# Branch C's output gate and a 512-column block of the output projection, each as seven quarter products with the tokens stationary

## The chip, the core and the metric

The kernel runs on one core of one Trainium2 chip. A core has five engines that run their own queues side by side: TensorE (PE, matrix products into the PSUM banks), VectorE (DVE), ScalarE (ACT), GpSimd (POOL) and SyncE (SP, which here issues the loads). Each engine takes its instructions strictly in the order in which the scheduler left them, and semaphores make one wait for another. The metric is the device time of the whole program in microseconds (us), the median of several executions.

## What is computed

Two layers, each a residual mixer over 512 tokens of width 1024. One input projection feeds four token mixers (branches A to D); each branch is multiplied by its own gate, projected up and merged by sigmoid gates; an output projection and a residual add follow. Cut to what matters here:

```
for l in range(2):
    h = rmsnorm(x, norm_g[l])                    # 512 x 1024
    proj = h @ w_in[l]                           # all branch inputs and gates
    c = sigmoid(o_raw) * mlstm(q, k, v, i, f)    # o_raw: 512 columns of proj, branch C's output gate
    c = headwise_rmsnorm(c) * silu(z_c)
    m = sum_n sigmoid(gate_n) * (y_n @ w_branch[l, n])
    x = x + m @ w_out[l]                         # 1024 x 1024
out = rmsnorm(x, final_g)
```

## The kernel before

Every product is done in float32r with both operands split in a high part (a rounding copy, on ScalarE) and a low part (the rest, a subtraction on VectorE). `mm3` issues three matmuls for it: high by high, high by low, low by high. Weights come in units of 128x1024 (512 KB) through `Stream`: a raw buffer `wr` (three of them), then the high part `wh` (line 283 or 257) and the low part `wl` (line 293 or 260), four buffers each. `Stream.get` keeps the loads five units ahead.

Three forms of product occur. `proj_W` (line 376) takes four units of 256 rows by 512 columns and accumulates four PSUM banks of 128 tokens by 512 columns: 4 units x 4 token tiles x 2 row tiles x 3 = 96 matmuls of 128x512. `proj_N` (line 359) does 256 columns with two units, 4 x 8 x 3 = 96 matmuls of 128x256. The merge gates already use seven quarter products (Strassen-Winograd): for these `split7` (line 249) makes the sums of the weight quarters on VectorE (lines 266 to 269), and `combine` (line 923) makes sums of the quarters of the normalised tokens, `bq`: T1, T2, T4 (split at lines 943 and 944) and T3 (written over a quarter of the tokens themselves by `in_place`, lines 955 and 956). Branch C's output gate runs as a `proj_W` on the four units of `co`, and `use_o` takes each of its banks in with one tanh on ScalarE (line 1001) and one update of `hC` on VectorE (line 1002). It comes behind branch D's q/k block and its v block (copied out at line 980), and `combine` runs beside it. The lines 1377 to 1422 are branch D: transposes, scores, products with the values.

The output projection takes the merged `mp` (split at lines 1058 and 1059) with a `proj_W` for columns 0 to 511 (taken in at line 1456) and two `proj_N` for the rest.

The order on each engine comes from the scheduler: program order, with the work under `high_priority` (weight casts, the taking in of results) put first, and side jobs released by `pump` as TensorE work is issued. Tiles come from pools (PSUM: four banks `pm`, four `px`), so a product also waits until the bank it takes has been read.

## Time and profile before

| | us |
|---|---|
| median of 3 runs (lowest to highest) | 1304.38 (1304.19 to 1304.83) |
| the profiled execution | 1304.66 |
| its span, first to last instruction | 1302.5 |
| TensorE busy in the span | 1294.3 (99%) |
| VectorE busy | 979.0 (75%) |
| ScalarE busy | 655.1 (50%) |
| granted TensorE clock, mean share of full | 0.999 |

In the timelines a row is: start in us from the start of the span, duration, engine, line of the kernel, operation, output and inputs by the program's names, shapes, count, and in brackets how long the engine had been idle and what released it. Instructions of one engine overlap a little, so the time that one takes in a full queue is the distance from start to start, not the duration. In the windows each engine has its busy time within the stretch, then the granted clock and what the transfers did.

### The profile page before, as it was taken

The page shows a single profiled execution, that of the slowest core. Times are in us where ns is not written, and L with a number is a line of the kernel's source. Part 1 is how long each engine was busy: PE and PEld are TensorE (multiplying, and loading weights), DVE is VectorE, ACT ScalarE, POOL GpSimd, SP SyncE. Part 2 cuts the span into 40 slices and gives each one's busy share as a digit, 9 for nine tenths or more (in the row PEclk, how much of TensorE's full clock was granted, in tenths as well). Part 3 has the DMA queues.
Part 4 walks back from the last instruction along what each step waited for, and adds up shares of the span by engine and source line. Part 5 has one row for each costly group of instructions (what it writes and reads, how often), then busy time and mean ns, then how long its engine had stood idle before and what let it go on. Part 6 is the DMA issues. An engine that isn't in the chain of part 4 may idle for free.

```text
span 1302.5 us, 20320 instructions
## 1 busy us (share of the span) xinstructions
PE 1294.3 (99%) x8044; PEld 1147.6 (88%) x8044; DVE 979.0 (75%) x1670; ACT 655.1 (50%) x1204; POOL 22.6 (2%) x35
## 2 busy tenths in 40 slices
PE   9999999999999999999999999999999999999998
PEld 9878888888999999998997788888889999999987
DVE  6676968876778797886476778798857787878855
ACT  6479323235457566454443973231454565764433
POOL 1000000000000001000000000000000000100000
PEclk9999999999999999999999999999999999999999
DMA  6222242211233233325432323332203233233341
GB/s 241 89 86 97 85 142 91 88 49 50 97 104 107 98 113 100 97 98 192 133 106 83 110 84 104 124 97 78 69 17 130 82 118 108 84 98 102 111 177 66
DMA packets 42191, 133.62 MB, mean 103 GB/s; under 512 B 5336, under 2 KB 5592, under 8 KB 42096
## 3 DMA queue, kind: packets, MB, share of 16 engines
q1 hardware_dynamic: 39504, 128.06, 29.3%
q10 hardware_dynamic: 2592, 4.27, 0.9%
q8 instruction: 63, 1.03, 0.3%
q14 instruction: 32, 0.26, 0.1%
HBM read 128.06 MB, written 4.24 MB: 102 GB/s over the span
## 4 chain that ended last, share of the span: by engine, by line
PE 95%; ACT 1%; DVE 1%; DMA 1%; issue 0%; POOL 0%; POOLq 0%; ACTq 0%
PE pm L337 23%; PE pm L338 23%; PE pm L339 23%; PE px L337 5%; PE px L339 5%; PE px L338 5%; PE px L1254 1%; DMA wr<-in_wu_dram 1%; PE px L1013 1%; PE px L1412 1%; ACT wh L257 1%; PE pm L543 1%; DVE wl L260 1%; PE px L1332 1%; PE px L1307 1%; PE px L1348 0%
## 5 line engine op out<-in xcount | busy, mean ns | idle before, releaser
L337 PE MATMUL pm<-hn,wh 128*128 128x512 f32 (+1 forms) x704 | 243.1, 345 | 0.0
L338 PE MATMUL pm<-hn,wh 128*128 128x512 f32 (+1 forms) x704 | 241.8, 344 | 0.0
L339 PE MATMUL pm<-hn,wl 128*128 128x512 f32 (+1 forms) x704 | 241.8, 343 | 0.0
L283 ACT CAST wh<-wr 128x1024 fp32r<-128x1024 f32 (+1 forms) x136 | 142.3, 1048 | 179.7 <-PE pm L339 75.1
L293 DVE TENSOR_TENSOR wl<-wr,wh 128x1024 fp32r<-128x1024 f32 (+1 forms) x136 | 166.1, 1223 | 79.8 <-ACT wh L283 79.7
L257 ACT CAST wh<-wr 128x1024 fp32r<-128x1024 f32 x120 | 125.3, 1047 | 110.5 <-DVE wr L268 72.1
L260 DVE TENSOR_TENSOR wl<-wr,wh 128x1024 fp32r<-128x1024 f32 x120 | 146.6, 1223 | 29.2 <-ACT wh L257 29.0
L337 PEld LDWEIGHTS pm<-hn,wh 128*128 128x128 f32 x704 | 132.5, 188 | 19.6 <-ACT cv L639 0.7
L338 PEld LDWEIGHTS pm<-hn,wh 128*128 128x128 f32 x704 | 132.6, 188 | 18.0 <-issue 0.4
L339 PEld LDWEIGHTS pm<-hn,wl 128*128 128x128 f32 x704 | 132.5, 188 | 16.8
L337 PE MATMUL pm<-wh,hn 128*128 128x512 f32 (+2 forms) x352 | 130.7, 372 | 0.0
L338 PE MATMUL pm<-wl,hn 128*128 128x512 f32 (+2 forms) x352 | 128.4, 365 | 0.0
L339 PE MATMUL pm<-wh,hn 128*128 128x512 f32 (+2 forms) x352 | 128.3, 365 | 0.0
L339 PE MATMUL pm<-yh,wl 128*128 128x512 f32 x256 | 101.1, 395 | 0.0
L337 PE MATMUL pm<-yh,wh 128*128 128x512 f32 x256 | 101.0, 394 | 0.0
L338 PE MATMUL pm<-yl,wh 128*128 128x512 f32 x256 | 100.9, 394 | 0.0
L337 PE MATMUL px<-T,wh 128*128 128x256 f32 x320 | 90.8, 284 | 0.9 <-ACT tg L1116 0.6
L339 PE MATMUL px<-T,wl 128*128 128x256 f32 x320 | 90.1, 281 | 0.0
L338 PE MATMUL px<-T,wh 128*128 128x256 f32 x320 | 89.8, 281 | 0.0
L339 PEld LDWEIGHTS pm<-wh,hn 128*128 128x128 f32 x352 | 66.2, 188 | 11.3
L338 PEld LDWEIGHTS pm<-wl,hn 128*128 128x128 f32 x352 | 66.3, 188 | 10.6 <-DVE wl L293 0.2
L337 PEld LDWEIGHTS pm<-wh,hn 128*128 128x128 f32 x352 | 66.2, 188 | 10.2
(352 smaller groups left out, 2834.2 us busy)
## 6 DMA issues: line engine op xcount, KB each, us to landing
wr<-in_wu_dram SPq DMA_DIRECT2D x212, 512.0 KB, 3.5
row<-rows SPq DMA_DIRECT2D x24, 256.0 KB, 4.1
x<-in_x_dram SPq DMA_DIRECT2D x15, 256.0 KB, 5.5
wr<-in_wz_dram SPq DMA_DIRECT2D x4, 544.0 KB, 4.6
xs<-x ACTq DMA_DIRECT2D x8, 256.0 KB, 2.6
x<-xs SPq DMA_DIRECT2D x8, 256.0 KB, 5.4
out_dram<-xo SPq DMA_DIRECT2D x4, 256.0 KB, 2.1
out_dram<-xo ACTq DMA_DIRECT2D x4, 256.0 KB, 2.5
```

What stands on the lines that cost most here:

```text
L257: A.copy(w[0], s)
L260: V.tensor_tensor(w[1], s, w[0].bitcast(F32), ALU.subtract)
L283: h = A.copy(hi, raw)
L293: d = V.tensor_tensor(lo, raw, hi.bitcast(F32), ALU.subtract)
L337: mm(ps, lh, rh, start=first, stop=False, **kw)
L338: mm(ps, lh, rl, start=False, stop=False, **kw)
L339: lastpm[0] = mm(ps, ll, rh, start=False, stop=last, **kw)
L543: pin(mm(bank[t][:, :272], xn[t, h][:, j * P:(j + 1) * P], ws.raw[h][:, 272 * j:272 * j + 272], start=h == 0 and j == 0, stop=h == 1 and j ...
L1013: nc.tensor.transpose(ps[:, t * P:(t + 1) * P], y[t][:, j * P:(j + 1) * P], ident)
L1254: mm(two(py, t)[:, 64 * e:64 * e + 64], M[e][:, t, :], xdt[t][:, o:o + 64], start=True, stop=True)
L1307: mm(ps[:, t], kT[h][:, s], qT[h][:, s], start=True, stop=True)
L1332: mm(pi[:, i], Ps[h][:, t], v1[t][:, h], start=True, stop=True)
```

## The change

The output gate of branch C and columns 256 to 767 of the output projection go through a new helper, `seven_w`. It views a 1024x512 block of weights as four quarters of 512x256 (one unit each, new unit kinds `in7w` and `out7w`) and the tokens as four quarters of 256 tokens by 512 rows, and computes seven products of 2 x 4 x 3 = 24 matmuls of 128x256, with the token quarters stationary. The four weight sums (S1 to S4) and all seven splits of weights are made inside it, from the raw units; before, four units were split as they came. X is one `px` bank used five times; three products add into what a bank holds already, and each partial result is taken in under high priority: a copy, then additions.

For the gate, the token sums are those of `combine`. For the projection, new sums of `md` (four subtractions of 128x256 for each of four row tiles) and their splits are made ahead of it. The projection's first 256 columns now come first as a `proj_N`, the middle 512 in seven products, the last 256 as a `proj_N` as before. There are four raw buffers `wr` in place of three, and four tiles `tm` in place of five. `in_place` comes right after `combine`, ahead of the gate.

The diff, cut to its core:

```
-    wide("dq", "dv", "co")
+    wide("dq", "dv")
+    wide7("in7w", OFF["co"])
...
-    for q in range(4):
-        u.append(("out4", 0, q))
-    for b in range(2, 4):
-        for h in range(2):
-            u.append(("out", 256 * b, h))
+    for h in range(2):
+        u.append(("out", 0, h))
+    wide7("out7w", 256)
+    for h in range(2):
+        u.append(("out", 768, h))
...
-    NTM = 5
+    NTM = 4
...
-                    raw = wp.tile([P, n], F32, name=nm("wr"), tag="wr", bufs=3)
+                    raw = wp.tile([P, n], F32, name=nm("wr"), tag="wr", bufs=4)
...
+    def seven_w(bq, acc):
+        a, b_, c_, d = ws.raw[-4:]
...
+        def part(n_, raw):
+            with tc.high_priority():
+                hi = wp.tile([P, 1024], F32R, name=nm("wh"), tag="wh", bufs=4)
+                lo = wp.tile([P, 1024], F32R, name=nm("wl"), tag="wl", bufs=4)
+                A.copy(hi, raw)
+                V.tensor_tensor(lo, raw, hi.bitcast(F32), ALU.subtract)
+            w[n_] = (hi, lo)
...
+        def product(ps, n_, t_, first):
+            for t in range(2):
+                for k in range(4):
+                    s, o = slice(t * P, (t + 1) * P), slice(k * 256, (k + 1) * 256)
+                    mm3(ps[:, t], bq[t_][0][k][:, s], bq[t_][1][k][:, s], w[n_][0][:, o], w[n_][1][:, o],
+                        first and t == 0 and k == 0, k == 3, skip_group_check=True)
...
+        part("A11", a)
+        sums(c_, c_, d, ALU.add)
+        sums(a, c_, a, ALU.subtract)
+        part("A12", b_)
+        sums(b_, b_, a, ALU.subtract)
+        part("S2", a)
+        part("S1", c_)
+        X = psx([P, 2, 256])
+        Y = [psm([P, 2, 256]) for _ in range(2)]
+        product(X, "A11", "B11", True)
+        take_in(0, 0, X, False)
+        sums(c_, d, a, ALU.subtract)
+        part("S3", c_)
+        product(Y[0], "A12", "B21", True)
+        take_in(0, 0, Y[0], True)
+        part("S4", b_)
+        product(X, "S2", "T2", False)
+        take_in(0, 1, X, False)
+        part("A22", d)
+        product(Y[1], "S1", "T1", True)
+        take_in(1, 1, Y[1], False)
+        product(X, "S3", "T3", False)
+        take_in(1, 1, X, True)
+        product(Y[1], "S4", "B22", False)
+        take_in(0, 1, Y[1], True)
+        product(X, "A22", "T4", False)
+        take_in(1, 0, X, True)
...
         for _ in steps:
             pass
+        in_place()
         yTA = halves(yA)
-        proj_W(hn, use_o)
+        seven_w(bq, use_o)
...
-        proj_W(mp, use_out0)
...
+        for k in range(4):
+            x, y = md[k], md[4 + k]
+            V.tensor_tensor(x[:, u0], x[:, u1], x[:, u0], ALU.subtract)
+            V.tensor_tensor(x[:, u1], y[:, u1], x[:, u1], ALU.subtract)
+            V.tensor_tensor(y[:, u1], y[:, u1], x[:, u0], ALU.subtract)
+            V.tensor_tensor(y[:, u0], y[:, u0], y[:, u1], ALU.subtract)
...
+        proj_N(mp, use_out0)
+        seven_w(bo, use_out7)
```

Where the instructions now stand, at three places of the first layer. First VectorE beside branch C's output gate, from the weight split that the anchor of the prediction is to the first T1. `bq` are the token sums, the T rows their low parts, `wl` low parts of weights, `qk` branch D's rotation, `to` and `hC` the gate's taking in. Before:

```order
408 L293 TENSOR_TENSOR wl_2504<-wr_2501,wh_2503 128x1024 [waits DMAHW2_49,PE_49,Activation_49]
409 L934 TENSOR_TENSOR bq_2541<-hn_120,hn_121 128x512
410 L938 TENSOR_TENSOR bq_2535<-bq_2537,bq_2535 128x512 [waits DVE_49]
411 L1383 TENSOR_TENSOR qk_2260<-qk_2260,cst_sb 128x256 [waits PE_49]
412 L938 TENSOR_TENSOR bq_2537<-bq_2541,bq_2537 128x512 [waits DVE_49]
413 L944 TENSOR_TENSOR T_491_2548<-bq_2535,T_490_2547 128x512 [waits Activation_49]
414 L938 TENSOR_TENSOR bq_2541<-bq_2541,bq_2535 128x512 [waits DVE_49]
415 L1383 TENSOR_TENSOR qk_2273<-qk_2273,cst_sb 128x256 [waits PE_49]
416 L938 TENSOR_TENSOR bq_2539<-bq_2539,bq_2541 128x512 [waits DVE_49]
417 L944 TENSOR_TENSOR T_493_2552<-bq_2541,T_492_2551 128x512 [waits Activation_49]
```
After (S3's weight sum stands one row ahead of this piece):

```order
413 L1005 TENSOR_TENSOR bq_2519<-bq_2521,bq_2519 128x512
414 L1464 TENSOR_TENSOR qk_2260<-qk_2260,cst_sb 128x256 [waits PE_49]
415 L1005 TENSOR_TENSOR bq_2521<-bq_2525,bq_2521 128x512 [waits DVE_49]
416 L329 TENSOR_TENSOR wl_2671<-wr_2457,wh_2670 128x1024 [waits Activation_49]
417 L1076 TENSOR_TENSOR to_2633<-to_2633,pm_2607 128x512 [waits PE_49]
418 L1023 TENSOR_TENSOR hn_121<-bq_2521,hn_120 128x2x256 [waits Activation_49]
419 L329 TENSOR_TENSOR wl_2712<-wr_2408,wh_2711 128x1024 [waits Activation_49]
420 L1083 SCALAR_TENSOR_TENSOR hC_2310<-to_2633,hC_2310 128x256 [waits Activation_49]
421 L269 TENSOR_TENSOR wal_2912<-wr_2901,wah_2911 128x512 [waits DMAHW3_49]
422 L1083 SCALAR_TENSOR_TENSOR hC_2378<-to_2633,hC_2378 128x256
423 L1005 TENSOR_TENSOR bq_2525<-bq_2525,bq_2519 128x512
424 L1011 TENSOR_TENSOR T_483_2532<-bq_2519,T_482_2531 128x512
```
T_491 before and T_483 after are the low part of T1's first half. Before, three rows of 512 and one of 256 stand between the weight split and it; after, S3's and S4's low parts, an accumulation `to`, two updates of `hC`, `in_place`'s row and the next merge gate's split stand there as well.

Second, TensorE where it first takes a token sum. Before, in the first merge gate:

```order
1314 L338 MATMUL pm_2940<-hn_121,wh_2674 128x256
1315 L339 MATMUL pm_2940<-hn_120,wl_2675 128x256
1316 L337 MATMUL pm_2941<-T_490_2547,wh_2678 128x256 [waits Activation_49]
1317 L338 MATMUL pm_2941<-T_491_2548,wh_2678 128x256
1318 L339 MATMUL pm_2941<-T_490_2547,wl_2679 128x256 [waits DVE_49]
```
After, in the middle of branch C's output gate:

```order
1257 L404 MATMUL px_2606<-wh_2598,T_484_2535 128x256 [waits Activation_49]
1258 L405 MATMUL px_2606<-wl_2599,T_484_2535 128x256
1259 L404 MATMUL pm_2608<-wh_2602,T_482_2531 128x256
1260 L405 MATMUL pm_2608<-wl_2603,T_482_2531 128x256
1261 L406 MATMUL px_2606<-wh_2598,T_485_2536 128x256 [waits DVE_49]
1262 L404 MATMUL px_2606<-wh_2598,T_484_2535 128x256
1263 L405 MATMUL px_2606<-wl_2599,T_484_2535 128x256
1264 L406 MATMUL px_2606<-wh_2598,T_485_2536 128x256
1265 L406 MATMUL pm_2608<-wh_2602,T_483_2532 128x256
1266 L404 MATMUL pm_2608<-wh_2602,T_492_2555 128x256 [waits Activation_49]
1267 L405 MATMUL pm_2608<-wl_2603,T_492_2555 128x256
1268 L406 MATMUL pm_2608<-wh_2602,T_493_2556 128x256 [waits DVE_49]
```
T_482 and T_483 are T1's first half, T_484 and T_485 T2's, T_492 and T_493 T1's second half. What stood behind the gate now stands inside it, with nothing else of TensorE's between.

Third, VectorE in the output projection, around the first taking in of results. Before:

```order
788 L293 TENSOR_TENSOR wl_6167<-wr_6164,wh_6166 128x1024 [waits DMAHW7_49,Activation_49]
789 L293 TENSOR_TENSOR wl_6197<-wr_6194,wh_6196 128x1024 [waits DMAHW0_49,Activation_49]
790 L293 TENSOR_TENSOR wl_6227<-wr_6224,wh_6226 128x1024 [waits DMAHW1_49,Activation_49]
791 L1456 TENSOR_TENSOR x_6141<-x_6141,pm_6160 128x512 [waits PE_49]
792 L1456 TENSOR_TENSOR x_6145<-x_6145,pm_6161 128x512 [waits PE_49]
793 L1456 TENSOR_TENSOR x_6149<-x_6149,pm_6162 128x512 [waits DMAHW3_49,PE_49]
```
After (px_6422 is the product A11, pm_6423 the product A12, wl_6415 the low part of S2, the wr rows the weight sums):

```order
830 L1544 TENSOR_TENSOR x_6228<-x_6228,px_6422 128x256 [waits PE_49]
831 L1544 TENSOR_TENSOR x_6232<-x_6232,px_6422 128x256
832 L334 TENSOR_TENSOR wr_6295<-wr_6295,wr_6297 128x1024 [waits DMAHW7_49,DMAHW0_49]
833 L334 TENSOR_TENSOR wr_6071<-wr_6295,wr_6071 128x1024 [waits DVE_49]
834 L1544 TENSOR_TENSOR x_6228<-x_6228,pm_6423 128x256 [waits PE_49]
835 L334 TENSOR_TENSOR wr_6160<-wr_6160,wr_6071 128x1024 [waits DVE_49]
836 L329 TENSOR_TENSOR wl_6415<-wr_6071,wh_6414 128x1024 [waits Activation_49]
837 L329 TENSOR_TENSOR wl_6419<-wr_6295,wh_6418 128x1024 [waits Activation_49]
```
Before, the weight splits stand ahead of all additions; after, the sums that S1 and S2 are made of stand behind additions that wait for TensorE.

## Rows read from the trace of the kernel before

**Rows 1.** Page: busy time, share of span, instructions; then the chain's shares by engine
```profile
PE 1294.3 (99%) x8044; PEld 1147.6 (88%) x8044; DVE 979.0 (75%) x1670; ACT 655.1 (50%) x1204; POOL 22.6 (2%) x35
...
PE 95%; ACT 1%; DVE 1%; DMA 1%; issue 0%; POOL 0%; POOLq 0%; ACTq 0%
```

**Rows 2.** Timeline of TensorE, output projection and ahead: start us, duration, line, shapes
```profile
603.80 0.28 PE L337 MATMUL px<-T,wh 128*128 128x256 f32 x1
...
605.22 0.40 PE L337 MATMUL pm<-yh,wh 128*128 128x512 f32 x1
...
608.01 0.39 PE L337 MATMUL pm<-wh,mph 128*128 128x512 f32 x1
...
630.21 0.28 PE L337 MATMUL pm<-wh,mph 128*128 128x256 f32 x1
```

**Rows 3.** Windows, first layer: length; PE, PEld, DVE, ACT, POOL busy; clock; transfers' share, GB/s
```profile
275.00:280.00 5.00, 5.00 (x27) 4.12 (x26) 1.94 (x4) 2.12 (x3) 0.00 (x0) 1.00 0.14 55
280.00:285.00 5.00, 5.00 (x28) 4.21 (x27) 5.00 (x10) 2.89 (x5) 0.00 (x0) 1.00 0.30 108
...
295.00:300.00 5.00, 5.00 (x23) 4.03 (x22) 4.90 (x8) 3.96 (x7) 0.00 (x0) 1.00 0.31 102
300.00:305.00 5.00, 5.00 (x35) 4.54 (x34) 5.00 (x8) 4.71 (x15) 0.00 (x0) 1.00 0.09 20
```

**Rows 4.** Timeline of VectorE, gate stage; last bracket: idle before, released by
```profile
278.13 1.23 DVE L293 TENSOR_TENSOR wl<-wr,wh 128x1024 fp32r<-128x1024 f32 x1 [3.06 <-ACT wh L283]
279.27 0.68 DVE L934 TENSOR_TENSOR bq<-hn,hn 128x512 f32<-128x512 f32 x1
...
280.48 0.42 DVE L1383 TENSOR_TENSOR qk<-qk,cst_sb 128x256 f32<-128x256 f32 x1
280.81 0.68 DVE L938 TENSOR_TENSOR bq<-bq,bq 128x512 f32<-128x512 f32 x1
281.42 0.68 DVE L944 TENSOR_TENSOR T<-bq,T 128x512 fp32r<-128x512 f32 x1
...
294.24 0.69 DVE L944 TENSOR_TENSOR T<-bq,T 128x512 fp32r<-128x512 f32 x1
...
299.19 1.29 DVE L944 TENSOR_TENSOR T<-bq,T 128x512 fp32r<-128x512 f32 x2
...
306.00 1.29 DVE L1389 TENSOR_TENSOR dqs<-dqT,cstd_sb 128x512 f32<-128x512 f32 x2 [0.70 <-ACT dqT L1379]
...
921.38 1.23 DVE L293 TENSOR_TENSOR wl<-wr,wh 128x1024 fp32r<-128x1024 f32 x1 [3.03 <-ACT wh L283]
```

**Rows 5.** Timeline of TensorE, gate stage, the same columns
```profile
276.36 0.40 PE L337 MATMUL pm<-wh,hn 128*128 128x512 f32 x1
...
279.17 1.47 PE L1377 MATMUL px<-cst_sb,qk 128*128 128x128 f32 x12
...
300.50 0.28 PE L337 MATMUL pm<-hn,wh 128*128 128x256 f32 x1
...
301.94 0.29 PE L337 MATMUL pm<-T,wh 128*128 128x256 f32 x1
...
307.95 0.49 PE L1412 MATMUL px<-vD,In 128*128 128x128 f32 x2
```

**Rows 6.** Timeline of ScalarE, gate stage, the same columns
```profile
276.56 0.59 ACT L980 COPY vD<-pm 128x512 f32<-128x512 f32 x1 [0.81 <-PE pm L339]
```

**Rows 7.** Windows, first layer, output projection, the same columns
```profile
615.00:620.00 5.00, 5.00 (x23) 4.05 (x22) 1.13 (x1) 0.65 (x1) 0.00 (x0) 1.00 0.35 111
620.00:625.00 5.00, 5.00 (x23) 4.03 (x22) 1.23 (x1) 0.48 (x2) 0.00 (x0) 1.00 0.33 111
```

**Rows 8.** End of the run: TensorE's last matmul, then two windows behind it
```profile
1296.25 0.28 PE L339 MATMUL pm<-wh,mpl 128*128 128x256 f32 x1
...
1297.00:1299.00 2.00, 0.00 (x0) 0.00 (x0) 1.12 (x3) 1.07 (x3) 0.55 (x1) 1.00 0.67 254
1299.00:1300.00 1.00, 0.00 (x0) 0.00 (x0) 0.00 (x0) 0.16 (x1) 0.00 (x0) 0.55 0.21 76
```

## What the change does to the time

> **What bounds the kernel now.** I read the page's busy shares and chain first [rows 1]. TensorE is busy for 99% of the span and 95% of the chain of work that ended last is its own, so one microsecond less of TensorE work is one microsecond less of time, as long as nothing else becomes late. Then I read the two stages that the change touches, in order of time, because VectorE's 75% is an average. From 280 to 305 us, which is the whole of branch C's output gate, VectorE is full: five windows of 5 us each hold 4.90 to 5.00 us of work [rows 3], while the window ahead has 1.94. In the output projection it has room: 1.13 and 1.23 of 5 us [rows 7]. The second layer runs the same code 643 us later (921.38 for 278.13 in [rows 4]), so each term is worked out for the first layer and taken twice.
>
> **TensorE's own work falls.** 96 matmuls of 128x512 run from 608.01 to 630.21, which is 0.2313 us each; 12 of 128x256 run from 603.80 to 605.22, 0.1183 each [rows 2]. Either stage goes from 96 x 0.2313 = 22.2 us to 7 x 24 = 168 matmuls x 0.1183 = 19.9 us. That is -2.3 us per stage, four times, -9.3 us in all if nothing waits. The other two column blocks of the projection keep their form and only change places.
>
> **Output gate: what moves.** The seven products need the token sums T1 to T4, which `combine` makes. Before, the first matmul with a T starts at 301.94 [rows 5], after the gate. Now it is the 49th of the gate's matmuls. In the trace of before, T1's low part is ready in two halves, at 281.42 and 294.24 (plus 0.68), and the second half of T2 only in the pair from 299.19 [rows 4]. So even the unchanged queue would hand T2 over as the gate ends. The new queue of VectorE is longer still, and in the first pair of order rows above, the low parts of the weight sums S3 and S4, an accumulation and two gate updates stand ahead of the first T1.
>
> I walk that queue with start-to-start times of back-to-back instructions: 1.14 us for 1024 elements (278.13 to 279.27), 0.61 for 512 (280.81 to 281.42), 0.33 for 256 (280.48 to 280.81) [rows 4]. The anchor is the low part at 278.13, which waits 3.06 us for ScalarE's cast; that cast stands behind the copy of branch D's last values at 276.56, which waits for TensorE [rows 6]. Its counterpart in the new queue stands behind the same copies, so I leave the anchor there. From it to T1's first half there are four instructions of 1024 elements, seven of 512 and three of 256: 4.6 + 4.3 + 1.0 = 9.9 us. T1's first half then starts at 288.0 and is done at 288.7, where before it started at 281.42. Ten more of 512 and two of 256, and one short wait of about 0.6 for ScalarE's cast between, lead to T1's second half, done near 295.9; T2's second half follows near 298.1.
>
> TensorE starts the gate at 276.36 and has the transposes of branch D (1.47 us) among its first products [rows 5]: A11 and A12 are 48 x 0.1183 = 5.7, so it is through at 276.36 + 5.7 + 1.5 = 283.5. Then it is in order: S1·T1 and S2·T2 (the second pair of order rows). It waits from 283.5 to about 289 for the first halves, works 12 matmuls (1.4 us), waits again until about 295 for the second half of T1, works 20 more, waits shortly for T2, and does the last 15. It is through at 298.1 + 15 x 0.1183 = 299.9. Of the 16.4 us, 48 matmuls are 5.7, so **about 10.7 us are waits**. S3·T3 adds into the bank that S2·T2 left, and has to wait for ScalarE's copy of it: by a copy's 0.59 [rows 6] and the end of the matmul, 1.0. Then 72 matmuls are 8.5. The stage ends at 309.4, where before the next one started at 300.50 [rows 5]: **+8.9**, the saving of 2.3 included.
>
> Behind it a smaller loss follows. The tanh of the last quarter, the casts of the next weights and the copies of branch D's transposes all stand behind the last product on ScalarE. Before, TensorE had 24 matmuls of 256 and 10 of 512 columns to do between 300.50 and branch D's scores; now 11 of them are free to run there. Walked the same way, branch D's next product, at 307.95 before [rows 5], starts 8.4 us later with 3.0 us less done ahead of it. So this costs 2.5 us more (bounds 0, and 5.2, all the work that stood there), and **the gate loses 11.4 us per layer**. The bounds are +7.2, the added length of VectorE's queue from the anchor to 306.00 (nine of 1024, 33 of 512, eleven of 256, 33.9 us by the rates above, against five, 33 and three, 26.7), and +14, with every wait at its end. The remaining weight sums stand earlier, where VectorE works 1.94 of 5 us just ahead of the gate [rows 3]; I cost them at nothing, and at 1 us where the load of the fourth unit would come late.
>
> **Clock.** The trace of before has one row on it: the last matmul starts at 1296.25, the granted clock is 1.00 in the window from 1297 to 1299 and 0.55 in the next [rows 8], so with TensorE idle it has gone from 2.4 towards 1.2 GHz. The first wait here is about 5.3 us and the second about 4, and either could end at the lower level. No matmul of before runs at the lower level, so I bound the price: 0 if the level is back before the last T arrives, since the slow matmuls ahead of that only fill a wait; 87 matmuls x 0.1183 = 10.3 us if it stays for the rest of the stage. I take the 15 matmuls after T2 at double time, **+1.8 per layer**, near the low end, since the slowed matmuls between the waits come for free. The Trainium skill's page "TensorE: Matmul & The Clock Gate", section "HAM oscillation — how this bites in real kernels", speaks against this change: groups of matmuls with waits between them each start at half rate. By it the full second and third group are slow, and the price nears the upper half of my bounds; no row of before shows it.
>
> **Output projection.** The 256-column block now comes first (96 x 0.1183 = 11.4 us from 608.01), then A11 and A12, to 625.1. VectorE has room, but its order counts (third pair of order rows): the sum of units c and d, two more sums and the splits of S2 and S1 stand behind additions that wait for A11 (622.2) and A12. From A11's end: two additions of 256, two sums of 1024 to about 625.6, ScalarE's cast of S2 to 627.0, that of S1 to 628.1, the low part of S2 to 628.4. TensorE, through with A12 at 625.4 after 0.35 for the last merged columns, starts S2·T2 in full at 628.4, some 2.9 us late with a few tenths more after it: +3.4 - 2.3 = **+1.1 per layer** (bounds -2.3, everything hidden, and +3). The splits of the token sums there lie beside the first block, in VectorE's free time.
>
> **The sum.** 11.4 + 1.8 + 1.1 = 14.3 per layer, 28.6 for two. The profiled execution took 1304.66 us, 0.3 over the median of the runs, so the forecast is 1304.7 + 28.6 = **1333 us**.
>
> **Rivals.** (a) *Only VectorE's added length counts*: if the waits for the T overlap with what came behind, the clock holds and the projection breaks even, the loss is 7.2 per layer: 1319. For it: TensorE has work of the next stage that needs no T. Against it: that work stands behind the products in TensorE's order. (b) *The clock stays low* after T2 in each gate stage, at 6.8 to 10.3 us per layer in place of 1.8: 1343 to 1350. For it speaks the row of the end [rows 8]; against it that after 298 matmuls run without long waits. By the rule of the Trainium skill's page named above, this is the case to expect. (c) *All of it is hidden*, and the time falls to 1304.7 - 9.3 = 1295. Place: the wait ahead of S1·T1. Its point is T1 and T2 complete by about 286 us, when TensorE gets to their second halves. The 281.42 of T1's first half in before speaks for it, the 294.24 and 299.19 of the second halves [rows 4] and the full windows [rows 3] against it. (d) *Gate and projection cancel out*: the projection gains its 4.6 and the gate loses about as much, near 1304. It needs a gate that loses 2 us per layer, below its lower bound.
>
> **How the numbers follow.** My forecast 0.55, (a) 0.20, (b) 0.13, (c) 0.08, (d) 0.04. The range reaches down to 1315, a little under (a), and up to 1349, most of (b). About 0.2% (2.6 us) is what a measurement can tell from no change. Faster by more: 0.08, within: 0.04, slower: 0.88.
>
> **What would show it.** TensorE's waits in the gate stage: two long ones on VectorE's T1 low part, of about 5 and 4 us, at 283 and 290 us and again 650 us later; first matmul of branch D's second product near 316; a granted clock below 1 just behind them; in the projection a wait of near 3 us ahead of S2·T2, released by ScalarE's cast. VectorE's windows from 280 to 310 full. If the waits for T1 are under 2 us, the walk of the queue is wrong, and with it the sign.

## The result, and the profile of the changed kernel

The changed kernel takes **1332.79 us** (median of 4 runs, 1332.28 to 1333.27) against 1304.29 for the kernel before in the same comparison (4 runs, 1303.89 to 1304.83). The ratio is 1.0218, with a 95% interval of 1.0202 to 1.0233. It is slower by 28.5 us; the forecast was 28.6. The profiled execution took 1332.83 us, with a span of 1330.9 and a mean granted clock of 0.987.

The page answers [rows 1] with busy time, share and count of each engine, and the chain's shares by engine:

```profile
PE 1299.1 (98%) x8332; PEld 1166.3 (88%) x8332; DVE 1037.9 (78%) x1780; ACT 676.7 (51%) x1238; POOL 22.5 (2%) x35
...
PE 93%; DVE 6%; ACT 1%; DMA 0%; issue 0%; POOLq 0%; POOL 0%
```

VectorE has gone from 1% to 6% of the chain that sets the end. TensorE's busy time is 4.8 us up, although its matmuls were to take 9.3 us less: part of them ran at the lower clock. And its idle time has gone up by 23.6 (28.4 of span less 4.8). The view of TensorE's waits says for whom (waiting operation and line, releaser and line: us in total, times, longest); the largest in the kernel before was 1.1:

```profile
PE pm L406 <- DVE T L1011: 9.7, 2, 4.9
PE pm L404 <- ACT T L1010: 6.3, 2, 3.2
PE px L404 <- ACT wh L328: 3.1, 2, 1.5
...
PE px L404 <- ACT to L1072: 1.4, 2, 0.7
PE pm L404 <- ACT wh L328: 1.1, 2, 0.6
PE px L1493 <- DVE In L1485: 0.9, 2, 0.5
```

The T are the token sums of the output gate; each wait occurs twice, once per layer. L328 is the cast of a weight sum; 2 x (1.5 + 0.6) us of waits on it belong to the output projection. Now TensorE's timeline in the gate of the first layer, which answers [rows 5] (start, duration, line, operands; in brackets the idle time before and its releaser):

```profile
283.84 0.28 PE L404 MATMUL pm<-wh,T 128*128 128x256 f32 x1
...
289.10 0.58 PE L406 MATMUL pm<-wh,T 128*128 128x256 f32 x1 [4.86 <-DVE T L1011]
...
294.90 0.58 PE L404 MATMUL pm<-wh,T 128*128 128x256 f32 x1 [3.16 <-ACT T L1010]
...
296.17 0.42 PE L404 MATMUL pm<-wh,T 128*128 128x256 f32 x1
296.39 0.41 PE L405 MATMUL pm<-wl,T 128*128 128x256 f32 x1
...
300.65 0.37 PE L404 MATMUL px<-wh,T 128*128 128x256 f32 x1
300.86 0.28 PE L405 MATMUL px<-wl,T 128*128 128x256 f32 x1
300.98 0.28 PE L406 MATMUL px<-wh,T 128*128 128x256 f32 x1
...
303.00 0.39 PE L404 MATMUL px<-wh,hn 128*128 128x256 f32 x1 [0.68 <-ACT to L1072]
...
311.64 0.28 PE L404 MATMUL pm<-hn,wh 128*128 128x256 f32 x1
...
318.33 0.49 PE L1493 MATMUL px<-vD,In 128*128 128x128 f32 x2 [0.45 <-DVE In L1485]
```

Two long waits at the T's, a short one for ScalarE's copy of S2·T2, and the gate ends at 311.64 where it ended at 300.50 before. Between 296.17 and 300.65 matmuls start 0.21 us apart, from 300.86 on 0.12: the first stretch ran at the lower clock. VectorE over the same time, which answers [rows 4]:

```profile
278.60 1.23 DVE L329 TENSOR_TENSOR wl<-wr,wh 128x1024 fp32r<-128x1024 f32 x1 [3.01 <-ACT wh L328]
...
288.37 0.68 DVE L1011 TENSOR_TENSOR T<-bq,T 128x512 fp32r<-128x512 f32 x1
...
295.06 0.68 DVE L1011 TENSOR_TENSOR T<-bq,T 128x512 fp32r<-128x512 f32 x1
...
297.47 0.68 DVE L1011 TENSOR_TENSOR T<-bq,T 128x512 fp32r<-128x512 f32 x1
```

After the anchor there is no bracket in these rows, so VectorE worked without a pause; T1's first half came at 288.37 because that is where it stood in the queue. The windows, which answer [rows 3] (length; busy time of PE, PEld, DVE, ACT, POOL; granted clock; transfers):

```profile
285.00:290.00 5.00, 0.90 (x4) 0.90 (x5) 5.00 (x9) 2.13 (x5) 0.00 (x0) 0.72 0.62 210
290.00:295.00 5.00, 1.84 (x9) 1.48 (x8) 5.00 (x10) 0.92 (x2) 0.00 (x0) 0.50 0.00 0
295.00:300.00 5.00, 4.90 (x21) 4.61 (x22) 3.84 (x7) 1.85 (x3) 0.00 (x0) 0.50 0.00 0
300.00:305.00 5.00, 4.32 (x33) 4.12 (x32) 2.41 (x3) 4.20 (x7) 0.00 (x0) 0.92 0.30 100
```

From 285 to 295 TensorE works 2.7 of 10 us while VectorE works all ten. Before, TensorE was full on both sides of this stretch [rows 3]. From 290 to 300 the granted clock is 0.50, the 1.2 GHz level.

To cut the 28.4 us into stages, the starts of the first and the last matmul with `mph` in the output projection, in both layers, are compared between profiles. Rows of after:

```profile
620.46 0.28 PE L404 MATMUL pm<-wh,mph 128*128 128x256 f32 x1
...
669.32 0.28 PE L405 MATMUL pm<-wl,mph 128*128 128x256 f32 x1
...
1277.28 0.28 PE L404 MATMUL pm<-wh,mph 128*128 128x256 f32 x1
...
1324.51 0.28 PE L405 MATMUL pm<-wl,mph 128*128 128x256 f32 x1
```

And of the kernel before, whose first one, 608.01, stands in [rows 2]:

```profile
654.32 0.28 PE L338 MATMUL pm<-wl,mph 128*128 128x256 f32 x1
...
1251.40 0.39 PE L337 MATMUL pm<-wh,mph 128*128 128x512 f32 x1
...
1296.13 0.28 PE L338 MATMUL pm<-wl,mph 128*128 128x256 f32 x1
```

The lag is 620.46 - 608.01 = 12.45 us when the first projection begins and 15.00 when it ends, so the first layer's gate with all behind it costs 12.45 and the projection 2.55. In the second layer it is 10.88 and 2.50. The same four rows, read in every run's profile, give this table (us; the experiments are told below):

| kernel | median, us | over before | to projection 1 | projection 1 | to projection 2 | projection 2 |
|---|---|---|---|---|---|---|
| the change | 1332.79 | 28.5 | +12.45 | +2.55 | +10.88 | +2.50 |
| e1 gate alone | 1328.81 | 24.3 | +12.17 | +0.12 | +11.75 | -0.14 |
| e2 projection alone | 1307.52 | 3.0 | -0.32 | +2.57 | -0.71 | +2.43 |
| e3 T1, T2 not waited for | 1329.79 | 25.3 | +10.23 | +2.58 | +9.66 | +2.48 |
| e8 no T waited for | 1324.31 | 19.9 | +9.05 | +3.70 | +8.57 | +1.24 |
| e4 wait filled | 1330.31 | 25.8 | +10.37 | +2.46 | +9.89 | +3.68 |
| e5 sums early | 1316.83 | 12.4 | +4.23 | +2.74 | +4.23 | +2.26 |
| e6 weight sums first | 1329.86 | 25.4 | +12.36 | +0.09 | +11.96 | +0.41 |
| e7 both orders | 1313.03 | 8.6 | +2.12 | +0.31 | +3.85 | +0.20 |
| e9 sums on GpSimd | 1321.39 | 17.0 | +9.71 | -0.46 | +9.08 | -1.22 |
| e10 projection alone, reordered | 1301.28 | -3.1 | -0.10 | -0.81 | -1.14 | -1.15 |
| e11 buffers alone | 1302.30 | -2.1 | -0.96 | 0.00 | -1.18 | +0.01 |

"Over before" is against the median of the kernel before in the same comparison (1304.29 to 1304.52); the four columns behind it are of one profiled execution each, which for e8 was 2.7 us above the median of its runs and for e7 2.1 below. The column to projection 1 also holds a lag from the first 17 us on, ahead of all that the change touches (0.56 us in the change, 0.20 to 0.60 in the experiments that keep a part of it, none in e11); its cause was not looked for.

### The profile page after: what moved, and what is told of

The parts are those of the page before. It is cut to its first block, busy times and chain, and to the rows that moved or that the text cites. A ratio compares the mean times of both kernels' runs of the same rounds, so it can differ in the third digit from the quotient of the medians.

```text
span 1330.9 us, 21031 instructions
## 1 busy us (share of the span) xinstructions
PE 1299.1 (98%) x8332; PEld 1166.3 (88%) x8332; DVE 1037.9 (78%) x1780; ACT 676.7 (51%) x1238; POOL 22.5 (2%) x35
## 4 chain that ended last, share of the span: by engine, by line
PE 93%; DVE 6%; ACT 1%; DMA 0%; issue 0%; POOLq 0%; POOL 0%
PE pm L406 21%; PE pm L404 21%; PE pm L405 21%; PE px L405 6%; PE px L404 6%; PE px L406 6%; PE px L1335 1%; PE px L1095 1%; DVE wl L329 1%; DVE wr L334 1%; PE px L1493 1%; PE pm L610 1%; DVE bq L1005 1%; PE px L1413 1%; PE px L1388 1%; DVE wl L269 1%
## 5 line engine op out<-in xcount | busy, mean ns | idle before, releaser
L292 ACT CAST wh<-wr 128x1024 fp32r<-128x1024 f32 (+1 forms) x120 | 125.6, 1048 | 124.4 <-issue 46.0
L302 DVE TENSOR_TENSOR wl<-wr,wh 128x1024 fp32r<-128x1024 f32 (+1 forms) x120 | 146.7, 1223 | 45.0 <-ACT wh L292 44.8
L404 PE MATMUL pm<-wh,hn 128*128 128x512 f32 (+2 forms) x320 | 114.2, 357 | 0.0
L405 PE MATMUL pm<-wl,hn 128*128 128x512 f32 (+2 forms) x320 | 112.3, 351 | 0.0
L406 PE MATMUL pm<-wh,hn 128*128 128x512 f32 (+2 forms) x320 | 112.3, 351 | 0.0
L406 PEld LDWEIGHTS pm<-wh,hn 128*128 128x128 f32 x320 | 60.2, 188 | 8.3
L405 PEld LDWEIGHTS pm<-wl,hn 128*128 128x128 f32 x320 | 60.3, 188 | 7.8 <-DVE wl L302 0.2
L404 PEld LDWEIGHTS pm<-wh,hn 128*128 128x128 f32 x320 | 60.2, 188 | 7.4
```

The lines of the kernel that those rows point to most:

```text
L292: h = A.copy(hi, raw)
L302: d = V.tensor_tensor(lo, raw, hi.bitcast(F32), ALU.subtract)
L404: mm(ps, lh, rh, start=first, stop=False, **kw)
L405: mm(ps, lh, rl, start=False, stop=False, **kw)
L406: lastpm[0] = mm(ps, ll, rh, start=False, stop=last, **kw)
```

## Experiments

The theory at this point: VectorE's queue hands the token sums over late, TensorE waits for them in order, and that costs most of the 28.5 us. The rivals: the lower clock is the larger part; or the gate and the projection share the loss otherwise than forecast; or the longer queue alone is the price, wherever the sums stand in it.

### One half at a time

e1 keeps the gate's seven products and undoes the projection's:

```
-    for h in range(2):
-        u.append(("out", 0, h))
-    wide7("out7w", 256)
...
+    for q in range(4):
+        u.append(("out4", 0, q))
...
+        proj_W(mp, use_out0)
```

> Only branch C's output gate is done in seven products; the output projection has its old form again (512 columns with 128x512 matmuls first, then twice 256). My theory puts most of the loss on the gate: the lag of the changed kernel behind the one before grows by 12.5 us in the first layer's gate stage and by 10.9 us in the second's, so this kernel should be near 1304.3 + 23.4 = 1327.7 us. Rival, that the two stages make each other worse (the raw weight buffers and loads they share): then this one is well under 1325 us.

Measured: 1328.81 us, ratio 1.0189 (1.0174 to 1.0204), 24.3 us over the kernel before. e2 does the opposite:

```
-    wide("dq", "dv")
-    wide7("in7w", OFF["co"])
+    wide("dq", "dv", "co")
...
-        seven_w(bq, use_o)
+        proj_W(hn, use_o)
```

> Only the output projection's middle 512 columns are done in seven products; branch C's output gate has its old form. My theory, from the lag that the changed kernel gains in the two projections (2.55 and 2.5 us): 1304.3 + 5.1 = 1309.4 us. As I predicted it before the clock was counted there (1.1 us per layer): 1306.5 us. Rival, that the projection alone gains its TensorE saving: 1304.3 - 4.6 = 1299.7 us.

Measured: 1307.52, ratio 1.0026 (1.0015 to 1.0037), 3.0 us over. So the gate carries some 24 and the projection some 3 us of the 28.5, and the two add up to about the whole (27.3; the small gain that e11 finds is in both). In the table the projection's stages cost 2.57 + 2.43 in e2 while the stretches ahead of them gain 0.32 + 0.71: something in e2 outside the projection is faster than before. e11 says what.

### Is it the wait for T, and which T?

In e3 the gate's products read B11 and B21 in place of T1 and T2, which are still computed.

```
-        seven_w(bq, use_o)
+        seven_w(dict(bq, T1=bq["B11"], T2=bq["B21"]), use_o)
```

> The changed kernel, but in branch C's output gate the products S1 and S2 read the plain token quarters B11 and B21 in place of the sums T1 and T2, so that part of the gate is another number; all sums are still made. It takes the wait for T1 and T2 away and leaves VectorE's queue as long as it was. If the wait is the cost: the two long waits of 4.9 and 3.2 us, the lower clock behind them (about 1.5 us) and the short wait for T2 go, and what remains is VectorE's longer queue, which then never waits for TensorE: some 5 to 7 us per layer in place of 11 to 12.5, 1318 to 1323 us. Rival, that the bank and its copies set the pace (one bank used five times): within 3 us of 1332.8. Rival, that nothing of VectorE's length remains once the wait is gone: 1305 us or less.

Measured: 1329.79, ratio 1.0195 (1.0180 to 1.0210): 25.3 us over, only 3.2 better than the change, where 10 to 15 were expected. The expectation missed, and TensorE's waits show why, in their view and in the timeline of the first layer:

```profile
PE px L404 <- ACT hn L1022: 15.5, 2, 7.8
...
302.56 0.58 PE L404 MATMUL px<-wh,hn 128*128 128x256 f32 x1 [7.75 <-ACT hn L1022]
```

The two waits of 4.86 and 3.16 have become one of 7.75 at S3·T3, whose T3 stands a little further down the same queue. The time alone would also fit the rival of the bank, but the wait names T3, and in e8 the same bank makes TensorE wait for nothing. (By the diff X takes four of the seven products, not five, and four products add into what their bank holds.) e8 therefore reads plain quarters for all four sums:

```
-        seven_w(bq, use_o)
+        seven_w(dict(bq, T1=bq["B11"], T2=bq["B21"], T3=bq["B22"], T4=bq["B22"]), use_o)
```

> As the run before that took T1 and T2 out of branch C's output gate, but now all four products with token sums (T1 to T4) read plain token quarters, so the gate is another number; the sums are still made for the merge gates. Without T1 and T2 alone the time fell by 3 us only, because TensorE then waited 7.8 us per layer for the second half of T3. If the token sums are the cost, all the waits in the gate stage go, TensorE is through the gate near 299.5 us, and what is left is VectorE's longer queue: some 4 to 6 us per layer, in all 1316 to 1323 us. Rival, that the seven products wait for weight sums and copies as much as for the token sums: within 4 us of 1329.8.

Measured: 1324.31, ratio 1.0149 (1.0132 to 1.0166), 19.9 us over and a microsecond outside what was expected. The gate has no wait and full clock now, yet 9.05 and 8.57 us per layer are left. The timeline of TensorE behind the gate, and two windows:

```profile
301.75 0.39 PE L404 MATMUL pm<-T,wh 128*128 128x256 f32 x1 [1.44 <-ACT wh L266]
...
305.88 0.58 PE L404 MATMUL pm<-T,wh 128*128 128x256 f32 x1 [1.65 <-ACT T L1010]
...
300.00:305.00 5.00, 1.56 (x9) 0.94 (x7) 5.00 (x6) 1.99 (x2) 0.00 (x0) 1.00 0.35 122
305.00:310.00 5.00, 2.27 (x7) 1.68 (x8) 5.00 (x11) 3.30 (x6) 0.00 (x0) 0.55 0.53 194
```

The next stage waits in its turn for weight splits and token sums, because VectorE still has all of its work to do: 5.00 of 5 us. Behind these waits the granted clock falls to 0.55, and the eight matmuls of 128x512 that start from 311.31 to 314.30 are 0.43 us apart in place of 0.23, which is 1.6 us of the 9.05. Taking one input away moves the wait to the next thing that VectorE hands over. This speaks for the rival that counts the length of the queue from there on, against the theory's first form, in which the T alone were late.

### What does the clock cost?

e4 puts 80 matmuls of 128x256, whose result nobody reads, between A12 and S2·T2 in the gate, so that TensorE doesn't stand still:

```
+            for j in range(fill):
+                mm(D_[:, 0:256], bq["B21"][0][j % 4][:, 0:P], w["A12"][0][:, 0:256], start=True, stop=True)
...
-        seven_w(bq, use_o)
+        seven_w(bq, use_o, 80)
```

> The changed kernel with 80 idle matmuls of 128x256 (9.5 us) added into a bank of its own in each gate stage, between the product A12 and the products with T2 and T1, where TensorE waits for VectorE. They change nothing that anybody reads. If the lower clock behind the waits costs about 1.5 us per layer, holding TensorE busy gives that back: 1332.8 - 3 = 1329.8 us, with the granted clock at 1.00 through the stage. Rival, that the clock costs nothing, because VectorE's queue is what sets the end of the stage: 1332.8 us, in spite of a clock of 1.00. If the added matmuls come in the way of real ones, it is slower than 1333.5 us.

Measured: 1330.31, ratio 1.0196 (1.0179 to 1.0213), 25.8 us over, so 2.7 less than the change although work was added. A window and a matmul of the first layer, to be held against 290 to 295 and 303.00 above:

```profile
290.00:295.00 5.00, 5.00 (x45) 5.00 (x44) 5.00 (x9) 1.97 (x3) 0.00 (x0) 1.00 0.00 0
...
300.97 0.39 PE L408 MATMUL px<-wh,hn 128*128 128x256 f32 x1 [0.68 <-ACT to L1076]
```

The granted clock is 1.00 where it was 0.50, and S3·T3 begins 2.0 us earlier. In the change 22 matmuls start 0.21 apart from 296.17 to 300.65, and at 0.21 in place of 0.12 they cost 2.1 us. VectorE still works 5.00 of 5 us, and most of the loss stays.

By the lags of the two gates the clock is worth 2.08 and 0.99 us. The price differs, since the change's clock came back sooner in the second layer. TensorE in the change there, at the end of the second wait and at the start of S3·T3:

```profile
952.75 0.58 PE L404 MATMUL pm<-wh,T 128*128 128x256 f32 x1 [3.16 <-ACT T L1010]
...
959.73 0.39 PE L404 MATMUL px<-wh,hn 128*128 128x256 f32 x1 [0.68 <-ACT to L1072]
```

That is 959.73 - 952.75 = 6.98 us, against 303.00 - 294.90 = 8.10 in the first layer. Ten matmuls start 0.21 apart, from 954.02 to 955.94, and cost 0.95.

By the medians, whose intervals overlap, e4 gains 2.7 in all; its second projection gives 1.18 back (3.68 in place of 2.50), with a granted clock of 0.50 from 1295 to 1300 where the change has 0.75. So the clock costs about 3 us in the gates, a tenth of the whole, and near a fifth with what it costs in the projections (some 1.3 each, told below): the rival that makes it the larger part falls.

### Does the order of VectorE's queue decide, or its length?

e5 spreads the same token sums over the projections of queries, keys and branch D's values ahead of the gate, where VectorE worked only 1.94 of 5 us at the end [rows 3]:

```
-    def proj_W(acts, consume):
+    def proj_W(acts, consume, also=None):
...
+                    if also:
+                        next(also, None)
...
+        steps = wait()
+        proj_W(hn, use_qk, steps)
...
+        proj_W(hn, lambda t, ps: A.copy(vD[t], ps), steps)
...
-        steps = combine()
```

> The changed kernel with the same result, but the token sums T1 to T4 are made step by step beside branch D's q/k and v blocks, ahead of the gate, where VectorE has some 10 us of room between 255 and 280; in VectorE's order all T rows now stand at most five rows behind the weight split that was my anchor. If their lateness is the cost: no wait for a T in the gate, and the gate stage at or up to 2 us under what it took before the change; with the projection's 5 us, 1305 to 1311 us. Rival, that VectorE's sum of work over both stages is the bound: branch C's recurrence is late instead and the gain is half, near 1320 us. Rival, no gain: 1333 us.

Measured: 1316.83, ratio 1.0092 (1.0077 to 1.0107), 12.4 us over: between the two expectations. The gate's stretch costs 4.23 in place of 12.45 and 10.88. So the order of the queue accounts for some 15 us, the clock's share in the long waits among them. The rest has moved ahead, to branch C's recurrence, whose state VectorE now hands over late (timeline of TensorE in e5):

```profile
277.83 0.38 PE L1427 MATMUL px<-stC,qT 128*128 128x129 f32 x1 [1.86 <-DVE stC L1442]
...
282.36 0.55 PE L404 MATMUL px<-wh,hn 128*128 128x256 f32 x1 [0.61 <-DVE dn L1449]
```

Part of this rest is again the clock: behind these waits it is 0.50 from 280 to 285, and the gate's matmuls start 0.21 apart until 285.70. In e7 (below), with waits of the same length for the state, it stays at 1.00 in the first layer, which costs 2.12, and falls to 0.55 from 925 to 930 in the second, which costs 3.85.

e6 turns one order round in the projection: the second weight sum goes ahead of the additions that wait for product A11.

```
+        second = sums(a, c_, a, ALU.subtract)
...
+        with tc.issue_after(second.ins):
+            take_in(0, 0, X, False)
```

> The changed kernel with the same result, but the taking in of the first product stands behind the first two weight sums in VectorE's order, in both stages. In the projection the sums then need not wait for TensorE's product A11: the waits of 1.5 and 0.6 us ahead of S2 and S1 and the lower clock behind them (1.4 us) go, and a projection costs 2.55 - 3.7 = -1.2 us: 1332.8 - 7.4 = 1325.4 us. If the loads of the weights, and not VectorE's order, make the sums late: 1332.8 us. The gate stage is not expected to change, since its two sums stand ahead already.

Measured: 1329.86, ratio 1.0194 (1.0179 to 1.0209), 25.4 us over: 3.1 of the 7.4 us that were expected. The projection itself loses 0.09 and 0.41 now in place of 2.5, so the order was its cause, but the second layer's stretch ahead of it is 1.1 us longer than in the change. That is the clock: from the end of the second wait to S3·T3 it is 8.08 us here (950.19 to 958.27), as in the first layer, where the change has 6.98. Two short waits are left (timeline of TensorE in e6):

```profile
638.62 0.39 PE L405 MATMUL px<-wh,Th 128*128 128x256 f32 x1 [0.52 <-DVE x L1545]
...
639.75 0.39 PE L406 MATMUL px<-wl,Th 128*128 128x256 f32 x1 [0.75 <-DVE wl L329]
```

The second: the low part of S2 stands behind A12's additions. e7 has both edits, e5's and e6's.

> Both of the last two edits in one kernel, with the same result as the reference. If the two stages are independent, the gains add up: 1297 to 1304 us, and with the gate at its best under the 1304.4 us of the kernel before. If VectorE is simply short of time over the two layers, no better than 1310 us.

Measured: 1313.03, ratio 1.0065 (1.0050 to 1.0080), 8.6 us over. The expectation, a gain, missed; its rival, no better than 1310 us, holds. With the same arithmetic on the same engines the order is worth 20 of the 28.5 us. The 8.6, and the 9.3 that the matmuls save, stay lost: TensorE waits for VectorE at branch C's state (5.5 us in two layers) and its denominator (2.7), and what the clock adds behind these waits differs from run to run. The four runs go from 1310.90 us with a mean granted clock of 0.997 to 1315.35 with 0.992.

### Moving the sums to an idle engine

GpSimd was busy for 2% of the span [rows 1]. e9 is e7 with the 16 token sums of each layer on GpSimd, and with e10's order of the weight sums (below):

```
-                        V.tensor_tensor(f[r, s], hn2[0].bitcast(F32)[o], hn2[1].bitcast(F32)[o], ALU.add)
+                        G.tensor_tensor(f[r, s], hn2[0].bitcast(F32)[o], hn2[1].bitcast(F32)[o], ALU.add)
...
-                    V.tensor_tensor(f[d], f[x], f[y], ALU.subtract)
+                    G.tensor_tensor(f[d], f[x], f[y], ALU.subtract)
```

> As the last kernel (token sums early, weight sums ahead of the first taking in), with the same result as the reference, and with two more edits: the 16 additions and subtractions of 128x512 that make T1 to T4 in each layer run on GpSimd, which is nearly idle, and in both stages the fourth weight sum and the taking in of the second product stand behind the splits of S2 and S1. It takes 16 x 0.6 = 9.7 us per layer off VectorE. If VectorE's time in the 50 us around the gate is the bound, the waits that went from the gate to branch C's state (1.9 + 0.9 + 1.4 us per layer, and a lower clock in some executions) go, and both stages gain what TensorE saves less about 1 us: 1296 to 1301 us, under both kernels. Rival, that GpSimd is too slow for it, or slows VectorE down while it works: the T are late again and it is 1313 us or more.

Measured: 1321.39, ratio 1.0132 (1.0116 to 1.0147), 17.0 us over: worse than e7, as the rival there said. The first layer at the time of the sums, GpSimd and VectorE in e9:

```profile
229.10 5.58 POOL L1006 TENSOR_TENSOR bq<-hn,hn 128x512 f32<-128x512 f32 x4
...
229.16 5.80 DVE L1376 TENSOR_SCALAR xd<-xd,brr 128x512 f32<-128x512 f32 x4 [0.91 <-POOL brr L476]
234.89 2.32 DVE L302 TENSOR_TENSOR wl<-wr,wh 128x1024 fp32r<-128x1024 f32 x1
```

and the same two operations of VectorE in e7, where GpSimd stands still:

```profile
228.76 1.67 DVE L1374 TENSOR_SCALAR xd<-xd,brr 128x512 f32<-128x512 f32 x4 [0.91 <-POOL brr L474]
230.36 1.22 DVE L302 TENSOR_TENSOR wl<-wr,wh 128x1024 fp32r<-128x1024 f32 x1
```

While GpSimd adds, four operations of VectorE take 5.80 us in place of 1.67, and one weight split 2.32 in place of 1.22. TensorE pays for it at branch C's scores (its waits in e9):

```profile
PE px L1398 <- DVE PC L1400: 16.3, 2, 8.2
```

### The projection alone, in a better order, and the bookkeeping alone

e10 is e2 (no seven products in the gate) with three moves: the first two weight sums ahead of A11's additions, A12's additions behind S1's low part, and the sum for S4 behind those.

```
-        sums(b_, b_, a, ALU.subtract)
...
+        with tc.issue_after(low.ins):
+            take_in(0, 0, Y[0], True)
+        sums(b_, b_, a, ALU.subtract)
```

> Only the output projection in seven products (branch C's output gate as before the change), with VectorE's order mended: the first two weight sums ahead of the taking in of A11, the taking in of A12 and the fourth weight sum behind the splits of S2 and S1; same result as the reference. The projection alone cost +3.0 us in all with the old order. If its waits (1.5 + 0.6 us per layer) and the lower clock behind them (1.4 us) came from the order of VectorE's queue, each projection now gains about 1 us against the kernel before: 1301 to 1303 us. If the loads make the sums late: 1307 us as before.

Measured: **1301.28** (10 runs, 1300.93 to 1301.72) against 1304.37, ratio 0.9977 (0.9967 to 0.9986): faster than both kernels, as expected. Two short waits of TensorE, 0.9 us in all, are left in its projection. But e2 had shown a gain outside it, so e11 takes the kernel before and changes only what the change does beside the products: the buffers, and a reciprocal square root written in place.

```
-    NTM = 5
+    NTM = 4
...
-                    raw = wp.tile([P, n], F32, name=nm("wr"), tag="wr", bufs=3)
+                    raw = wp.tile([P, n], F32, name=nm("wr"), tag="wr", bufs=4)
...
-            r = small("hr", [P, NT, 4])
-            rsqrt(r.rearrange("p t h -> p (t h)"), ss.rearrange("p t h -> p (t h)"), mul, 4 * NT)
+            r, v = ss, ss.rearrange("p t h -> p (t h)")
+            rsqrt(v, v, mul, 4 * NT)
```

> The kernel before with only the change's bookkeeping: four raw weight buffers in place of three, four tiles of the tm pool in place of five, and the square root taken in place; no seven products. In the profile of the reordered projection alone (1301.3 us) 1.2 of the 3.2 us that its span gains lie outside the two projections. If they are the fourth raw buffer's, this kernel is at 1303.2 us; if they come with the seven products or are scatter, at 1304.4 us.

Measured: 1302.30 against 1304.42, ratio 0.9983 (0.9974 to 0.9992): 2.1 us faster with no product changed, a little more than expected. The profile puts it ahead of the two projections (-0.96 and -1.18), not in them, and behind the gates, in the merge gates that follow (the last table below). Which of the three edits brings it wasn't tried. Of e10's 3.1 us, 2.1 would then be the buffers and 1.0 the seven products; the two intervals overlap, so the split is what the medians say and no more. In e10's profile the projections do gain 0.81 and 1.15 us, against an ideal of 2.3 each, and TensorE is 0.8 us late there ahead of the first gate already.

## Why the prediction was right, and where it was not

**VectorE's queue in the gate: right, in its steps too.** The walk gave T1's first half a start of 288.0 (288.37 measured), its second half an end near 295.9 (295.74), T2's second half 298.1 (298.15). TensorE was to reach the T's at 283.5 (283.84) and to wait about 5 and 4 us (4.86 and 3.16, and more within the groups). The stage was to end at 309.4 plus 1.8 for the clock, 311.2 (311.64), and branch D's product to start 8.4 + 1.8 = 10.2 us later (318.33 against 307.95 in [rows 5], 10.4). The wait for ScalarE's copy was put at 1.0; from the last matmul of S2·T2 to the first of S3·T3 it is 303.00 - 302.05 = 0.95. Three us of work were to be left undone ahead of branch D's product; behind that stretch the lag is 13.19 (table below), 2.8 more than 10.4. The sign near 316 us for that product leaves the prediction's own 1.8 for the clock out.

**The clock: right in kind, its size partly luck.** The level fell in the first wait and was 0.50 from 290 to 300. The ten matmuls before the second wait ran at 0.21 us and came for free, since they only shortened the wait that followed. The prediction priced 15 matmuls behind T2, at 1.8 per layer. Measured are 22 behind T1's second half in the first layer, 2.1 us, and ten in the second, 0.95; the short wait for T2 did not come, since the slow matmuls ahead of it lasted to 299.80 and T2 was complete at 298.15. In both layers together it is 3.1 by the lags of e4's gates, against 3.6 in the sum. When the level comes back was a choice within wide bounds and no reading, and the two layers show that it can come at either time. The rule of the Trainium skill's page "TensorE: Matmul & The Clock Gate", section "HAM oscillation — how this bites in real kernels", holds for the two groups behind the long waits, which start at half rate (0.21 us). The group behind the wait of 0.68 runs at 0.12 us from its second matmul on, so the price stayed at the low end of the bounds.

**The projection: the term was too small.** It was put at +1.1 per layer and measured +2.55 and +2.50. The step was right, weight sums behind additions that wait for A11: VectorE's row on these additions waits for the product, the sum behind it follows, and TensorE waits twice:

```profile
635.09 0.75 DVE L1544 TENSOR_TENSOR x<-x,px 128x256 f32<-128x256 f32 x2 [1.81 <-PE px L406]
635.76 1.22 DVE L334 TENSOR_TENSOR wr<-wr,wr 128x1024 f32<-128x1024 f32 x1
...
639.42 0.38 PE L404 MATMUL px<-wh,Th 128*128 128x256 f32 x1 [1.54 <-ACT wh L328]
640.37 0.38 PE L404 MATMUL pm<-wh,Th 128*128 128x256 f32 x1 [0.56 <-ACT wh L328]
...
642.00:647.00 5.00, 5.00 (x31) 5.00 (x31) 3.25 (x6) 3.67 (x5) 0.00 (x0) 0.66 0.45 157
```

The two waits are 2.1 us. From the end of A12 at 637.72 to 641.11, where matmuls follow one another again, with three of them done between, TensorE loses 3.0, about the 2.9 of the prediction. What it left out was the lower clock here: it is 0.66 in the window from 642 to 647, and 15 matmuls at 0.21 from 642.18 to 645.37 cost 1.4 us. That is the 1.4 by which the term was missed. e8, whose edit does not touch the projection, shows the two parts: with the same two waits (1.54 and 0.56) in both layers, its second projection has the clock at 1.00 throughout and costs 1.24, near the 1.1 of the prediction, and its first has 0.50 from 637 to 642 and costs 3.70. e6 and e10, whose waits are shorter, keep the full clock there and lose next to nothing, or gain.

**The bookkeeping: costed at nothing, and a gain.** The prediction counted the fourth raw buffer only as a possible loss of 1 us. e11 has it, with the other two edits, 2.1 us faster.

**So the sum came out partly by errors that cancel.** TensorE's matmuls of a run can be matched one by one with those of the kernel before. Their median lag (us) in six stretches, each given in times of the kernel before:

| kernel | 200 to 262, ahead of gate 1 | 350 to 385, behind it | 500 to 600 | 810 to 890, ahead of gate 2 | 1000 to 1030, behind it | 1145 to 1240 |
|---|---|---|---|---|---|---|
| the change | 0.58 | 13.19 | 12.47 | 15.15 | 26.89 | 26.02 |
| e6 weight sums first | 0.49 | 13.09 | 12.38 | 12.59 | 25.44 | 24.55 |
| e11 buffers alone | -0.08 | -0.19 | -0.95 | -0.89 | -1.04 | -2.13 |

The gates with the clock cost 12.61 and 11.74, together 24.4, where 2 x 13.2 = 26.4 was forecast. Behind them the change regains 0.72 and 0.87, in the stretches where e11 gains 0.76 and 1.09, so the bookkeeping is worth about 1.6 inside the change as well, where 0 was forecast. The projections cost 5.0 in place of 2.2, and 0.6 is there from the start. That is 24.4 - 1.6 + 5.0 + 0.6 = 28.4 against 28.6: the gates were put 2.0 too high and the projections 2.8 too low, and the bookkeeping, less the 0.6, takes back the difference.

The prediction took two equal layers, and the change's second gate is 0.87 cheaper than its first. That is the clock, which came back 12 matmuls sooner there, worth 1.1 us. In e6, where it came back as late in both layers, the gates cost 12.60 and 12.85.

**The rivals.** (a), VectorE's added length alone, 1319: not the case here, since TensorE had nothing to do in the waits. But e8 shows that it was the nearest to what lies beneath: with every T at hand, 9.05 us of the 12.45 come back in the next stage, and without the 1.6 that the clock took there it is 7.4, where (a) has 7.2 per layer. (b), the clock staying low: the level was back at 300.86 us, and at 956.30 in the second layer. (c), all hidden, needed T1 and T2 by 286 us; T2 was complete at 298.15. (d) needed a gate that loses 2 us, and even e7's loses 2.12 and 3.85.

## What to carry to other kernels

Seven products in place of eight take time from TensorE and give work to VectorE, and in the gate, where VectorE is full already, the exchange cost more than it brought in each order tried: find the stage's windows of the engine that receives the work before anything else. Late inputs are found by walking the receiving engine's queue instruction by instruction from an anchor in the trace; taking one late input away only moves the wait to the next one (T1, then T3, then the next stage's splits), while moving the sums to where the engine has room took away more than half of the loss, and two thirds with the weight sums in a better order. Compare stages between two profiles only with the granted clock beside them: the same waits cost 1 us more or less here, by when the clock came back. And time apart what a change does in passing, its buffers and temporaries: here that was at least half of the only gain there was.

## What the runs showed of the hardware

VectorE's operations became slower while GpSimd ran additions of 128x512: 5.80 us in place of 1.67 for four multiplications by a scalar, 2.32 in place of 1.22 for a weight split. GpSimd itself took 1.5 us on average, with VectorE at work beside it, for a sum that takes VectorE 0.6. The Trainium skill's page "SBUF — State Buffer", section "Who interferes with whom", names a port pair that the two engines take as an exclusive lock; the four multiplications, which end as GpSimd's four sums do (234.96 and 234.68), are in line with it, but no run here tells a lock from a slower sharing.

The granted clock also fell in the projection, behind waits of only 1.5 and 0.6 us with few matmuls between them, where the prediction had counted on the full level. And the same stall did not always bring the same price: in the two layers of one run 22 and ten matmuls ran at the lower level behind equal waits (3.16 us each), and in e8 the projection's second occurrence kept the full clock where the first had 0.50.
